# Down projection's S1 begun in gate and up, additions kept in order, residual rows loaded into place, the norm's second block scaled on VectorE

## The chip, the cores and the metric

One core of one Trainium2 chip runs the program. Its engines are TensorE (PE; its weight loads are shown as PEld), VectorE (DVE), ScalarE (ACT), GpSimd (POOL) and SyncE (SP). The first four compute; SP and POOL also start the DMAs that matter here. The metric is the device time of one execution in microseconds: 1347.09 us before the change, the median of 3 runs (1346.76 to 1351.79).

## The reference

Two decoder layers on x of shape (1, 512, 1024), all float32:

```
for each layer:
    p = x @ w_in                          # columns for two token mixers
    a = gated linear recurrence (4 heads x 128)
    b = sparse attention (8 heads x 64: compressed, selected and window branch)
    x = layer_norm(alpha*x + concat(a, b) @ w_out, ln1)
    h = silu(x @ w_ffn_gate) * (x @ w_ffn_up)        # 512 x 2816
    x = layer_norm(alpha*x + h @ w_ffn_down, ln2)    # alpha = sqrt(2)
```

The layer norm takes mean and variance over the 1024 columns, and then multiplies by a vector g and adds a vector b.

## The kernel before

Every matmul operand is split into a high and a low float32r half (a cast on ScalarE, then a subtraction on VectorE), and a product is three matmuls: high by high, high by low, low by high (`mm3`). The order of the instructions on each engine is fixed when the program is built: a planner walks a modelled timeline and takes, on each engine, the ready instruction of the highest priority, giving out the buffers of each tag as they come free. `high_priority(offset=3000)` moves an instruction ahead by 3000 places. On the chip every engine, and every DMA queue, then works in that fixed order.

The 512 rows stand as four tiles `rows[0]` to `rows[3]` of 128 x 1024, in two large buffers `R` (tag `a`, 11 buffers of 128 x 2048).

Output projection (`first_half`, `second_half`): the first half adds alpha times the old rows. Line 887 loads them in eight pieces of 128 x 512 into small tiles `xr` (tag `f`, three buffers), and line 888 scales them, adds PSUM and writes `rows`. `second_half` splits its third weight into two more buffers of `f`.

Norm (`norm_turn`): for two row tiles at a time, `norm_stats` gives the mean and 1/deviation, line 735 their product, and ScalarE scales both tiles in place (line 736). TensorE transposes them, and ScalarE applies g and b on the way to the next layer's operands (line 745). The rows themselves get g and b later, in `norm_rest`: a multiplication and an addition of 128 x 1024 for each of four tiles (lines 756 and 757). In gate and up this hangs on hook 3 of `seven`.

Gate and up (`seven`): twenty units, each two weight blocks combined with the halves of x by Strassen's scheme in seven products of 12 matmuls. `stage` loads a unit's weights with SyncE into tiles `a` (128 x 1024), `s1`, `s3` and `d`, and GpSimd adds to `s1` and `s3` by accumulating DMAs (lines 104 and 105). Tile `a` takes tag `wr` (two buffers), in every third unit `f` (in the third unit `pt`). Line 117 subtracts for the low halves, line 153 and line 162 make two more sums on VectorE.

Down projection: Strassen again, over four quarters q of the hidden columns. `first(q)` needs the sum S1 of two weight blocks: a load by SyncE (line 1036; line 1060 for q = 3) and an addition by GpSimd's queue (line 1038; 1061). Line 1074 adds a third block to the same tile for `third(q)`, and line 1087 a fourth for `fourth(q)`. The final loop needs one more sum, S3, in a buffer of `f` (line 1128), which comes free when the S1 tile that had it is done. GpSimd's queue takes all these additions in turn, each when its own load has landed and its readers are done.

Of the kernel before, what the change touches and what calls it, by code (L numbers as in the profile page):

```python
# [34 lines left out]
class Kern:  # L35
# [58 lines left out]
    def stage(self, sa, sb):  # L94

        nc = self.nc
        with self.tc.high_priority(offset=3000):
            self.turn += 1
            tag, bufs = ("wr", 2) if self.turn % 3 else ("pt", 2) if self.turn == 3 else ("f", 3)
            a = self.sb.tile([128, 1024], F32, name="wraw", tag=tag, bufs=bufs)  # L100
            s1, s3, d = (self.sb.tile([128, 512], F32, name=n, tag=t, bufs=2) for n, t in (("ws1", "st"), ("ws3", "pc"), ("wd", "wd")))
            nc.sync.dma_start(s1, sb[:, 512:])
            nc.sync.dma_start(s3, sa[:, :512])
            nc.gpsimd.dma_start(s1, sb[:, :512], accum_op=OP.add)
            nc.gpsimd.dma_start(s3, sb[:, :512], accum_op=OP.add)
            nc.sync.dma_start(a, sa)
            nc.sync.dma_start(d, sb[:, 512:])
        return a, s1, s3, d
# [17 lines left out]
    def seven(self, units, R, hooks):  # L126

        nc = self.nc
# [11 lines left out]
        for n, unit in enumerate(units + [None]):  # L140
# [8 lines left out]
            if unit:  # L149
                self.prod(D, s1, R["T1"], True)  # L150
                y = copy("sy", D)
                with self.tc.high_priority(offset=3000):
                    nc.vector.tensor_tensor(a[:, :512], s1, a[:, :512], op=OP.add)
                self.prod(B, a[:, 512:], R["R21"], True)
                unit[2]("11", B, x)
# [64 lines left out]
    def wide_mm(self, pts, w, xs, i, start, stop, by_tile=False):  # L220

        order = [(k, t) for k in range(2) for t in pts]
        if by_tile:
            order.sort(key=lambda kt: list(pts).index(kt[1]))
        for k, t in order:
            self.mm3(pts[t], *xs(2 * i + k, t), *w(k * 512, 512), start and k == 0, stop and k == 1)

    def xs_of(self, x):
# [499 lines left out]
    def norm_turn(self, l, which, b, rows, x, raw=None):  # L728
# [3 lines left out]
        for t in (2 * b, 2 * b + 1):  # L732
            mean, rs = self.norm_stats(t)
            nb = self.small(1, "nb", tag="l")
            nc.vector.tensor_scalar(nb, mean, rs, -1.0, op0=OP.mult, op1=OP.mult)
            nc.scalar.activation(rows[t], rows[t], AF.Identity, scale=rs, bias=nb)
        for k2 in range(0, NK, 2):
# [24 lines left out]
    def layer(self, l):  # L762
# [95 lines left out]
        def rblocks():  # L858
            R.extend(self.big("r") for _ in range(2))
            rows.extend(R[t // 2].rearrange("p a b -> p (a b)")[:, (t % 2) * 1024:(t % 2 + 1) * 1024] for t in range(NT))  # L860

        def quart(b, q):
# [13 lines left out]
        def first_half(c):  # L876

            def f():
                ws = [self.load_w(io["wo1"][l, c, i]) for i in range(2)]
                cs = slice(c * 512, (c + 1) * 512)  # L880
                for b in range(2):
                    pts = {t: self.ps("d") for t in (2 * b, 2 * b + 1)}
                    for i in range(2):
                        self.wide_mm(pts, ws[i], ysf, i, i == 0, i == 1)
                    xr = self.sb.tile([128, 2, 512], F32, name="xr", tag="f", bufs=3)
                    for e, (t, p) in enumerate(pts.items()):
                        nc.gpsimd.dma_start(xr[:, e], self.xres[t * 128:(t + 1) * 128, cs])
                        nc.vector.scalar_tensor_tensor(rows[t][:, cs], xr[:, e], ALPHA, p, op0=OP.mult, op1=OP.add)
            return f
# [115 lines left out]

        self.seven([(io[w][l, j], io[w][l, j + 1], f(j)) for j in range(2, NF, 2) for w, f in (("wg", gate), ("wu", up))], R,
                   {3: lambda: self.norm_rest(l, 0, rows, None)})

# [7 lines left out]
        def split(dst, src):  # L1016
            with tc.high_priority(offset=3000):
                nc.scalar.copy(dst[0], src)  # L1018
                nc.vector.tensor_tensor(dst[1], src, dst[0].bitcast(F32), op=OP.subtract)  # L1019

        def places(k):
# [11 lines left out]

        def raw_w(src, plus=None, tag=("wr", 2)):
            t = self.sb.tile([128, 1024], F32, name="wraw", tag=tag[0], bufs=tag[1])
            nc.sync.dma_start(t, src)
            if plus is not None:
                nc.gpsimd.dma_start(t, plus, accum_op=OP.add)
            return t

        def dprod(acc, w, r, start, stop):
# [8 lines left out]
        half = [[(H[2 * q + e][:, :, b * 256:(b + 1) * 256]) for e in range(2) for b in range(2)] for q in range(QS)]  # L1050
        sums, ops = {}, {}

        def first(q):

            with tc.high_priority(offset=3000):
                if q < 3:
                    s = raw_w(wd[1, 2 * q], wd[1, 2 * q + 1], ("f", 3))
                else:
                    s = self.big("ws").rearrange("p a b -> p (a b)")[:, :1024]
                    nc.sync.dma_start(s, wd[1, 2 * q])  # L1060
                    nc.gpsimd.dma_start(s, wd[1, 2 * q + 1], accum_op=OP.add)
            r11, r12, _, r22 = half[q]
# [6 lines left out]
            with tc.high_priority(offset=3000):  # L1069
                nc.vector.scalar_tensor_tensor(r11, t1, -1.0, r22, op0=OP.mult, op1=OP.subtract)  # L1070
            sums[q] = s
            dprod(Y, split_w(s), o1, q == 0, q == QS - 1)
            with tc.high_priority(offset=3000):
                nc.gpsimd.dma_start(s, wd[0, 2 * q], accum_op=OP.add)

# [5 lines left out]
        def third(q):  # L1081
# [4 lines left out]
            with tc.high_priority(offset=3000):  # L1086
                nc.gpsimd.dma_start(sums[q], wd[0, 2 * q + 1], accum_op=OP.add)

        def fourth(q):
            dprod(Z, split_w(sums[q]), ops["22", q], q == 0, q == QS - 1)  # L1090

        for f, q in ((first, 0), (first, 1), (second, 0), (first, 2), (third, 0), (second, 1), (first, 3), (third, 1),
                     (fourth, 0), (second, 2), (third, 2), (fourth, 1), (second, 3), (third, 3), (fourth, 2)):
            f(q)
# [28 lines left out]
        for q in range(QS):  # L1123
# [3 lines left out]
            with tc.high_priority(offset=3000):  # L1127
                s3 = raw_w(wd[0, i], wd[1, i], ("f", 3))
                p12, p22 = raw_w(wd[0, i + 1]), raw_w(wd[1, i + 1])
                nc.vector.tensor_tensor(r12, r22, r12, op=OP.subtract)  # L1130
# [5 lines left out]
            split(o4, r11)  # L1136
            dprod(Q, split_w(s3), o3, q == 0, end)
            dprod(M, split_w(p12), o21, False, False)
            if q == 0:
                fourth(QS - 1)  # L1140
            dprod(N, split_w(p22), o4, q == 0, end)
            if q == 0:
# [149 lines left out]
```

## Time and profile before

| | |
|---|---|
| median of 3 runs | 1347.09 us |
| the profiled execution | 1353.65 us |
| its span, first to last instruction | 1351.9 us |
| TensorE busy, share of the span | 1311.2 us, 97% |
| VectorE | 1012.4 us, 75% |
| ScalarE | 749.6 us, 55% |
| GpSimd | 192.5 us, 14% |
| mean granted TensorE clock | 0.989 of 2.4 GHz |
| moved by DMA | 186.54 MB, 138 GB/s |

Matmuls overlap, so a recorded matmul is longer than the step from one to the next, and a busy TensorE need not be at its peak. In the tables and chains below, "x" counts instructions, `out<-in` names tiles, and "<-" behind an idle time names what ended it. Layer 0 has gate and up from about 350 to 557 us and the down projection until about 670; layer 1 has them from about 1020 to 1227 and until the end.

### The profile page before, as it was taken

The page shows a single profiled execution, that of the slowest core. Times are in us where ns is not written, and L with a number is a line of the kernel's source. Part 1 is how long each engine was busy: PE and PEld are TensorE (multiplying, and loading weights), DVE is VectorE, ACT ScalarE, POOL GpSimd, SP SyncE. Part 2 cuts the span into 40 slices and gives each one's busy share as a digit, 9 for nine tenths or more (in the row PEclk, how much of TensorE's full clock was granted, in tenths as well). Part 3 has the DMA queues.
Part 4 walks back from the last instruction along what each step waited for, and adds up shares of the span by engine and source line. Part 5 has one row for each costly group of instructions (what it writes and reads, how often), then busy time and mean ns, then how long its engine had stood idle before and what let it go on. Part 6 is the DMA issues. An engine that isn't in the chain of part 4 may idle for free.

```text
span 1351.9 us, 23468 instructions
## 1 busy us (share of the span) xinstructions
PE 1311.2 (97%) x8853; PEld 1200.4 (89%) x8853; DVE 1012.4 (75%) x2021; ACT 749.6 (55%) x1495; POOL 192.5 (14%) x275
## 2 busy tenths in 40 slices
PE   8999999999999999999999999999999999999997
PEld 6988999789999999877899989987899999997776
DVE  4755798866887778967667668988559877788767
ACT  5254777844655555645452558777256555556530
POOL 1140111111011121110011100111010111111102
PEclk9999999999999999999999999999999999999999
DMA  7253212252467778586433221132515777866852
GB/s 236 79 164 102 79 56 74 84 161 76 149 167 185 189 189 197 136 223 174 152 140 116 73 92 63 63 102 71 166 29 179 178 184 180 215 158 150 213 196 79
DMA packets 67682, 186.54 MB, mean 138 GB/s; under 512 B 8175, under 2 KB 8351, under 8 KB 67056
## 3 DMA queue, kind: packets, MB, share of 16 engines
q1 hardware_dynamic: 44640, 124.73, 27.9%
q0 software_dynamic: 21920, 58.47, 21.2%
q10 hardware_dynamic: 1008, 1.84, 0.4%
q8 instruction: 69, 1.13, 0.3%
q14 instruction: 45, 0.37, 0.1%
HBM read 180.76 MB, written 7.10 MB: 139 GB/s over the span
## 4 chain that ended last, share of the span: by engine, by line
PE 59%; DVE 5%; DMA 5%; ACT 2%; issue 2%; POOL 0%; POOLq 0%; DVEq 0%; ACTq 0%
PE ps_d L83 10%; PE ps_d L82 10%; PE ps_d L84 10%; PE ps_t L84 3%; PE ps_t L82 3%; PE ps_t L83 3%; DMA wraw<-in_wd 3%; PE ps_s L82 2%; PE ps_s L83 2%; PE ps_s L84 2%; DMA ws<-in_wd 1%; PE ps_t L647 1%; DVE wlo L1019 1%; DVE hop L1019 1%; PE ps_h L390 1%
## 5 line engine op out<-in xcount | busy, mean ns | idle before, releaser
L116 ACT CAST whi<-wraw 128x512 fp32r<-128x512 f32 x160 | 98.6, 620 | 123.1 <-PE ps_d L83 93.3
L82 PE MATMUL ps_d<-xh,whi 128*128 128x256 f32 (+1 forms) x424 | 141.9, 338 | 2.0 <-ACT gates L497 1.2
L84 PE MATMUL ps_d<-xh,wlo 128*128 128x256 f32 (+1 forms) x424 | 142.6, 337 | 0.0
L83 PE MATMUL ps_d<-xl,whi 128*128 128x256 f32 (+1 forms) x424 | 141.7, 335 | 0.6 <-DVE mv L712 0.6
L117 DVE TENSOR_TENSOR wlo<-wraw,whi 128x512 fp32r<-128x512 f32 x160 | 108.9, 687 | 44.5 <-ACT whi L116 42.1
L84 PE MATMUL ps_d<-th,wlo 128*128 128x256 f32 x480 | 133.7, 284 | 2.4 <-DVE wlo L117 2.4
L83 PE MATMUL ps_d<-tl,whi 128*128 128x256 f32 x480 | 134.9, 283 | 0.0
L82 PE MATMUL ps_d<-th,whi 128*128 128x256 f32 x480 | 133.9, 283 | 0.1
L76 ACT CAST whi<-wraw 128x1024 fp32r<-128x1024 f32 (+1 forms) x68 | 70.7, 1040 | 97.0 <-PE ps_d L84 19.8
L77 DVE TENSOR_TENSOR wlo<-wraw,whi 128x1024 fp32r<-128x1024 f32 (+1 forms) x68 | 82.4, 1211 | 51.9 <-ACT whi L76 51.5
L84 PEld LDWEIGHTS ps_d<-th,wlo 128*128 128x128 f32 x480 | 91.2, 192 | 3.0 <-DVE wlo L117 3.0
L83 PEld LDWEIGHTS ps_d<-tl,whi 128*128 128x128 f32 x480 | 92.1, 192 | 0.1
L82 PEld LDWEIGHTS ps_d<-th,whi 128*128 128x128 f32 x480 | 91.4, 192 | 0.9 <-ACT su L136 0.5
L82 PEld LDWEIGHTS ps_d<-xh,whi 128*128 128x128 f32 x424 | 81.4, 193 | 9.2 <-ACT gates L497 1.3
L1019 DVE TENSOR_TENSOR wlo<-wraw,whi 128x1024 fp32r<-128x1024 f32 x50 | 60.6, 1219 | 38.3 <-ACT whi L1018 38.3
L83 PEld LDWEIGHTS ps_d<-xl,whi 128*128 128x128 f32 x424 | 81.9, 193 | 7.6 <-DVE mv L712 1.2
L84 PEld LDWEIGHTS ps_d<-xh,wlo 128*128 128x128 f32 x424 | 81.8, 193 | 7.5 <-DVE wlo L77 0.5
L83 PE MATMUL ps_d<-wlo,xh 128*128 128x256 f32 (+1 forms) x304 | 88.3, 291 | 0.0
L82 PE MATMUL ps_d<-whi,xh 128*128 128x256 f32 (+1 forms) x304 | 88.0, 291 | 0.0
L1018 ACT CAST whi<-wraw 128x1024 fp32r<-128x1024 f32 x50 | 52.3, 1051 | 64.1 <-DMA wraw<-in_wd 38.9
L84 PE MATMUL ps_d<-whi,xl 128*128 128x256 f32 (+1 forms) x304 | 87.8, 290 | 0.0
L608 ACT ACTIVATE e<-e,mn 128x128 f32<-128x128 f32 (+3 forms) x128 | 71.8, 564 | 22.1 <-DVE mn L606 21.7
(460 smaller groups left out, 4182.1 us busy)
## 6 DMA issues: line engine op xcount, KB each, us to landing
wraw<-in_wd SPq DMA_DIRECT2D x50, 512.0 KB, 4.2
wraw<-in_wf SPq DMA_DIRECT2D x31, 512.0 KB, 3.2
wraw<-in_wd POOLq DMA_DIRECT2D x26, 512.0 KB, 6.7
wraw<-in_wg SPq DMA_DIRECT2D x24, 512.0 KB, 3.9
wraw<-in_wu SPq DMA_DIRECT2D x24, 512.0 KB, 4.6
ws<-in_wg SPq DMA_DIRECT2D x40, 256.0 KB, 3.7
ws<-in_wg POOLq DMA_DIRECT2D x40, 256.0 KB, 4.7
ws<-in_wu SPq DMA_DIRECT2D x40, 256.0 KB, 3.6
```

What stands on the lines that cost most here:

```text
L76: nc.scalar.copy(h, raw[:, i:i + n])
L77: nc.vector.tensor_tensor(o, raw[:, i:i + n], h.bitcast(F32), op=OP.subtract)
L82: first = t.matmul(out, ah, bh, start=start, stop=False, **kw)
L83: t.matmul(out, ah, bl, start=False, stop=False, **kw)
L84: t.matmul(out, al, bh, start=False, stop=stop, **kw)
L116: nc.scalar.copy(h, raw)
L117: nc.vector.tensor_tensor(o, raw, h.bitcast(F32), op=OP.subtract)
L390: nc.tensor.matmul(p2[:, i], S[:, blk(i)], kq(128 * (i + 2), [[2 * w, n], [256 + w, 2], [1, w]]), start=True, stop=True)
L608: nc.scalar.activation(e, e, AF.Exp, bias=mn, scale=-1.0, accum_out=sm)
L647: nc.tensor.transpose(p[:, c:c + 128], E[qt][:, j * 128:(j + 1) * 128], self.ident)
L1018: nc.scalar.copy(dst[0], src)
L1019: nc.vector.tensor_tensor(dst[1], src, dst[0].bitcast(F32), op=OP.subtract)
```

## The change

Five edits:

- `seven` no longer uses the tag `f`: tile `a` is in `wr` in all units but the third. `stage` keeps its last SyncE load, its last GpSimd addition and (from line 153) its VectorE sum in `self.tail`.
- The S1 sums of the down projection are begun by hooks of `seven`: the load of quarter q at unit 10 + 2q, its addition one unit later, placed in their queues behind those of the unit before by a new function `after` (an order, no wait). Quarter 3 uses a large buffer.
- The norm's remainder in gate and up becomes eight single instructions, one at each of units 3 to 9 and one at unit 11 (a multiplication and an addition for each tile in turn), each behind the VectorE sum of the unit before. The parameters are loaded at unit 2.
- All additions to the sums keep the order of the program on GpSimd's queue, and S3 is in large buffers of its own, two quarters to a buffer; it is begun by `begin3`: quarters 0 and 1 before `fourth(0)` and `fourth(1)`, the others in the final loop.
- The residual rows are loaded into `rows` by four DMAs of 128 x 1024, in place of eight pieces; line 888 then works in place. In `norm_turn` the scalings get a high priority, and the second tile of block 0 is scaled by VectorE.

```diff
@@ stage
-            tag, bufs = ("wr", 2) if self.turn % 3 else ("pt", 2) if self.turn == 3 else ("f", 3)
-            a = self.sb.tile([128, 1024], F32, name="wraw", tag=tag, bufs=bufs)
+            tag = "pt" if self.turn == 3 else "wr"
+            a = self.sb.tile([128, 1024], F32, name="wraw", tag=tag, bufs=2)
...
-            nc.gpsimd.dma_start(s3, sb[:, :512], accum_op=OP.add)
+            add = nc.gpsimd.dma_start(s3, sb[:, :512], accum_op=OP.add)
             nc.sync.dma_start(a, sa)
-            nc.sync.dma_start(d, sb[:, 512:])
+            self.tail = [nc.sync.dma_start(d, sb[:, 512:]), add, None]
@@ seven
-                    nc.vector.tensor_tensor(a[:, :512], s1, a[:, :512], op=OP.add)
+                    self.tail[2] = nc.vector.tensor_tensor(a[:, :512], s1, a[:, :512], op=OP.add)
+    def after(self, a, b):
+        self.tc.add_manual_dep(a.ins, b.ins.name, mybir.DependencyInfo(
+            mybir.DependencyClass.NoSync, mybir.DependencyReason.DATA), reason="queue order")
@@ norm_turn
-            nc.vector.tensor_scalar(nb, mean, rs, -1.0, op0=OP.mult, op1=OP.mult)
-            nc.scalar.activation(rows[t], rows[t], AF.Identity, scale=rs, bias=nb)
+            with self.tc.high_priority(offset=4000):
+                nc.vector.tensor_scalar(nb, mean, rs, -1.0, op0=OP.mult, op1=OP.mult)
+                if b == 0 and t % 2:
+                    nc.vector.tensor_scalar(rows[t], rows[t], rs, nb, op0=OP.mult, op1=OP.add)
+                else:
+                    nc.scalar.activation(rows[t], rows[t], AF.Identity, scale=rs, bias=nb)
@@ rblocks, first_half
+            for t in range(NT):
+                nc.gpsimd.dma_start(rows[t], self.xres[t * 128:(t + 1) * 128, :])
...
-                    xr = self.sb.tile([128, 2, 512], F32, name="xr", tag="f", bufs=3)
-                    for e, (t, p) in enumerate(pts.items()):
-                        nc.gpsimd.dma_start(xr[:, e], self.xres[t * 128:(t + 1) * 128, cs])
-                        nc.vector.scalar_tensor_tensor(rows[t][:, cs], xr[:, e], ALPHA, p, op0=OP.mult, op1=OP.add)
+                    for t, p in pts.items():
+                        o = rows[t][:, cs]
+                        nc.vector.scalar_tensor_tensor(o, o, ALPHA, p, op0=OP.mult, op1=OP.add)
@@ gate and up, down projection
-                   {3: lambda: self.norm_rest(l, 0, rows, None)})
+        def add_w(t, src):
+            d = nc.gpsimd.dma_start(t, src, accum_op=OP.add)
+            self.after(d, self.tail[1])
+            self.tail[1] = d
...
+        def begin(q):
+            sums[q] = self.sb.tile([128, 1024], F32, name="wsum", tag="f", bufs=3) if q < 3 else halves("ws")[0]
+            self.after(nc.sync.dma_start(sums[q], wd[1, 2 * q]), self.tail[0])
+        def go_on(q):
+            add_w(sums[q], wd[1, 2 * q + 1])
+        def rest(i):
+            r, c = rows[i // 2], i % 2 * 1024
+            self.after(nc.vector.tensor_tensor(r, r, lnps[0][:, c:c + 1024], op=OP.add if i % 2 else OP.mult), self.tail[2])
+        hooks = {10 + 2 * q + e: lambda q=q, f=f: f(q) for q in range(QS) for e, f in enumerate((begin, go_on))}
+        hooks[2] = lambda: lnps.append(self.ln_params(l, 0))
+        for i in range(2 * NT):
+            hooks[i + 3 if i < 7 else 11] = lambda h=hooks.get(i + 3 if i < 7 else 11, lambda: None), i=i: (h(), rest(i))
...
-                nc.gpsimd.dma_start(s, wd[0, 2 * q], accum_op=OP.add)
+                add_w(sums[q], wd[0, 2 * q])
...
-                nc.gpsimd.dma_start(sums[q], wd[0, 2 * q + 1], accum_op=OP.add)
+                add_w(sums[q], wd[0, 2 * q + 1])
+        def begin3(q):
+            if q % 2 == 0:
+                s3s.extend(halves("ws3"))
+            with tc.high_priority(offset=3000):
+                nc.sync.dma_start(s3s[q], wd[0, 2 * q])
+                add_w(s3s[q], wd[1, 2 * q])
-                     (fourth, 0), (second, 2), (third, 2), (fourth, 1), (second, 3), (third, 3), (fourth, 2)):
+                     (begin3, 0), (fourth, 0), (second, 2), (third, 2), (begin3, 1), (fourth, 1), (second, 3), (third, 3),
+                     (fourth, 2)):
...
-                s3 = raw_w(wd[0, i], wd[1, i], ("f", 3))
+            if q < QS - 2:
+                begin3(q + 2)
```

## Rows read from the trace of the kernel before

**Rows 1.** Windows: us, busy of each engine (count), granted clock, DMA share, GB/s.

```profile
375.00:545.00 170.00, 170.00 (x1419) 170.00 (x1418) 133.92 (x240) 95.48 (x196) 30.16 (x35) 1.00 0.76 188
553.00:656.00 103.00, 98.77 (x441) 79.75 (x441) 78.93 (x100) 51.57 (x66) 12.32 (x15) 0.98 0.75 193
```

**Rows 2.** TensorE's waits, whole span: total us, times, longest us.

```profile
PE ps_t L82 <- ACT whi L1018: 5.7, 3, 2.2
...
PE ps_d L82 <- DVE r L888: 2.9, 2, 2.3
...
PE ps_s L82 <- ACT whi L1018: 1.6, 3, 0.6
```

**Rows 3.** TensorE's waits from 355 to 375 us, gate and up of layer 0.

```profile
PE ps_t L82 <- ACT whi L116: 0.9, 1, 0.9
PE ps_d L84 <- DVE wlo L117: 0.8, 1, 0.8
PE ps_t L84 <- DVE wlo L117: 0.6, 1, 0.6
```

**Rows 4.** TensorE's waits from 1028 to 1052 us, gate and up of layer 1.

```profile
PE ps_d L84 <- DVE wlo L117: 1.6, 2, 1.2
PE ps_t L82 <- DVE h_at L978: 1.1, 1, 1.1
```

**Rows 5.** Timeline of VectorE from 360 us: start us, us, instruction, count.

```profile
361.05 4.62 DVE L756 TENSOR_TENSOR r<-r,lnp 128x1024 f32<-128x1024 f32 x4
365.59 0.68 DVE L162 TENSOR_TENSOR wraw<-wraw 128x512 f32<-128x512 f32 x1
```

**Rows 6.** Timeline of TensorE from 606 us, around the hole before `fourth(3)`.

```profile
607.45 0.40 PE L84 MATMUL ps_o<-whi,hop 128*128 128x512 f32 x1
...
612.35 0.63 PE L83 MATMUL ps_t<-wlo,hop 128*128 128x512 f32 x1
```

**Rows 7.** Timeline of GpSimd from 568 us, the additions of the down projection.

```profile
571.17 0.86 POOL L1087 DMA_DIRECT2D wraw<-in_wd  x1 [1.76 <-DVE wlo L1019]
...
598.09 0.85 POOL L1038 DMA_DIRECT2D wraw<-in_wd  x1 [10.09 <-DMA wraw<-in_wd]
598.63 1.20 POOL L1087 DMA_DIRECT2D ws<-in_wd  x1
```

**Rows 8.** Timeline of VectorE from 590 us, the split of quarter 3's sum.

```profile
592.19 1.23 DVE L1019 TENSOR_TENSOR wlo<-ws,whi 128x1024 fp32r<-128x1024 f32 x1 [0.89 <-ACT whi L1018]
```

**Rows 9.** Timeline of ScalarE from 575 us, the splits for `fourth(0)` and `fourth(3)`.

```profile
579.24 1.04 ACT L1018 CAST whi<-wraw 128x1024 fp32r<-128x1024 f32 x1 [4.64 <-DMA wraw<-in_wd]
...
608.76 1.04 ACT L1018 CAST whi<-ws 128x1024 fp32r<-128x1024 f32 x1 [5.78 <-DMA ws<-in_wd]
```

**Rows 10.** Windows of 3.4 us behind the wait for line 888.

```profile
962.20:965.60 3.40, 1.33 (x5) 1.09 (x6) 3.17 (x4) 0.16 (x1) 0.00 (x0) 0.92 0.24 59
965.60:969.00 3.40, 3.40 (x12) 2.68 (x11) 1.26 (x2) 1.04 (x1) 0.00 (x0) 0.57 0.73 249
```

**Rows 11.** Timeline of VectorE from 950 us, first half of the output projection.

```profile
962.39 1.23 DVE L77 TENSOR_TENSOR wlo<-wraw,whi 128x1024 fp32r<-128x1024 f32 x1 [5.36 <-ACT whi L76]
963.53 0.68 DVE L888 SCALAR_TENSOR_TENSOR r<-xr,ps_d 128x512 f32<-128x512 f32 x1
```

**Rows 12.** Timeline of ScalarE from 950 us, same place.

```profile
955.21 1.05 ACT L76 CAST wx<-wraw 128x1024 fp32r<-128x1024 f32 x1 [1.89 <-DVE r L888]
```

**Rows 13.** Groups by line and form, ScalarE: busy us, mean ns, idle before.

```profile
L736 ACT ACTIVATE r<-r,nb,rstd 128x1024 f32<-128x1024 f32 x12 | 14.9, 1244 | 18.6 <-DVE nb L735 18.3
```

**Rows 14.** Groups by line and form, VectorE.

```profile
L345 DVE TENSOR_SCALAR hgF<-hgF,lbv 128x512 f32<-128x512 f32 x4 | 2.2, 545 | 3.2 <-ACT hgF L342 3.2
```

**Rows 15.** Line 106 from 380 to 545 us, the loads of `a`.

```profile
DMA to landing us min/median/max: 3.5/5.0/6.3
```

**Rows 16.** Line 116 from 380 to 545 us: what ended its idle time, longest.

```profile
  PE ps_d L83: 50.1, 47
```

**Rows 17.** Timeline of SyncE's queue from 545 us.

```profile
556.07 0.33 SPq L1060 DMA_DIRECT2D ws<-in_wd  x1
```

More of the change, by code (lines that the diff above doesn't have):

```diff
@@ L1004, in up @@
             return take
-        self.seven([(io[w][l, j], io[w][l, j + 1], f(j)) for j in range(2, NF, 2) for w, f in (("wg", gate), ("wu", up))], R,
-                   {3: lambda: self.norm_rest(l, 0, rows, None)})
         QS = 4
@@ L1019, in split, with raw_w, halves @@
                 nc.vector.tensor_tensor(dst[1], src, dst[0].bitcast(F32), op=OP.subtract)
+        def raw_w(src):
+            t = self.sb.tile([128, 1024], F32, name="wraw", tag="wr", bufs=2)
+            nc.sync.dma_start(t, src)
+            return t
+        def add_w(t, src):
+            d = nc.gpsimd.dma_start(t, src, accum_op=OP.add)
+            self.after(d, self.tail[1])
+            self.tail[1] = d
+        def halves(name):
+            b = self.big(name).rearrange("p a b -> p (a b)")
+            return [b[:, :1024], b[:, 1024:]]
+        sums = {}
+        def begin(q):
[3 more added lines that the diff above has]
+            add_w(sums[q], wd[1, 2 * q + 1])
+        lnps = []
+        def rest(i):
[5 more added lines that the diff above has]
+            hooks[i + 3 if i < 7 else 11] = lambda h=hooks.get(i + 3 if i < 7 else 11, lambda: None), i=i: (h(), rest(i))
+        self.seven([(io[w][l, j], io[w][l, j + 1], f(j)) for j in range(2, NF, 2) for w, f in (("wg", gate), ("wu", up))], R, hooks)
         def places(k):
@@ L1032, in split_w @@
             return w
[L1034 to L1039, printed above, removed]
         def dprod(acc, w, r, start, stop):
@@ L1050, in layer @@
         half = [[(H[2 * q + e][:, :, b * 256:(b + 1) * 256]) for e in range(2) for b in range(2)] for q in range(QS)]
-        sums, ops = {}, {}
+        ops, s3s = {}, []
         def first(q):
[L1055 to L1061, printed above, removed]
             r11, r12, _, r22 = half[q]
@@ L1070, in first @@
                 nc.vector.scalar_tensor_tensor(r11, t1, -1.0, r22, op0=OP.mult, op1=OP.subtract)
-            sums[q] = s
-            dprod(Y, split_w(s), o1, q == 0, q == QS - 1)
+            dprod(Y, split_w(sums[q]), o1, q == 0, q == QS - 1)
             with tc.high_priority(offset=3000):
-                nc.gpsimd.dma_start(s, wd[0, 2 * q], accum_op=OP.add)
+                add_w(sums[q], wd[0, 2 * q])
         def second(q):
@@ L1136, in layer @@
             split(o4, r11)
-            dprod(Q, split_w(s3), o3, q == 0, end)
+            dprod(Q, split_w(s3s[q]), o3, q == 0, end)
             dprod(M, split_w(p12), o21, False, False)
```

## The prediction

> **What bounds the kernel now.** I read the table by stage first. In gate and up, TensorE and its weight loads are both busy for the whole stretch, 1419 matmuls in 170.0 us or 0.120 us each, at the full 2.4 GHz level [rows 1]; nothing can be gained there, only lost. VectorE is at 133.9 of these 170 us, the DMA engines at a share of 0.76. In the down projection TensorE has 4.2 us of recorded idle time in 103 [rows 1]. The list of TensorE's waits then says what is late when it stops: the high half of a weight in the down projection (5.7 and 1.6 us), the eviction of line 888 (2.9 us) [rows 2], and early in gate and up the splits of lines 116 and 117, 2.3 us in layer 0 and 2.7 us in layer 1 [rows 3, 4]. So the change can win only by closing such holes, some 13 us of waits, and what a hole drags behind it: after the one at 962 us the granted clock of the next 3.4 us is 0.57, so most of it ran at 1.2 GHz [rows 10]. The two slices lose (0.08 + 0.43) x 3.4 = 1.7 us.
>
> **The sum** is made against the profiled execution, 1353.65 us (span 1351.9, and 1.75 around it). It lies 0.49% above the median of 1347.09, so the forecast is scaled by the ratio at the end.
>
> *The norm's remainder, spread over gate and up.* Before, eight VectorE instructions per layer (four multiplications, four additions, 128x1024) come nearly together: four take 4.62 us from 361.05, and the sum of line 162, which a split and then TensorE need, starts only at 365.59 [rows 5]. That is where the 2.3 us of layer 0 come from; layer 1 has the same pattern. Now one of the eight follows each of eight blocks. A block is 84 matmuls of 0.120 = 10.1 us; VectorE does 133.9/170 of that, 7.9 us, and with 1.2 us more 9.1, still under 10.1. Gain at most 2.3 + 2.7 = 5.0 us; if every layer has one addition fall ahead of a late split instead, -2.4 us. I take 4.5, near the top, because the work around is otherwise unchanged. The load of the norm's parameters is issued one block ahead of its first reader; its cover is that block.
>
> *S1 begun in gate and up, S3 in buffers of its own, additions in order.* The S1 sums of quarters 0 to 2 were already loaded in gate and up, in buffers of the tag `f`. Only quarter 3's was not: SyncE issues its load at 556.07 [rows 17]. The larger effect is at the other end. Quarter 3's sum is read for the third product by 592.19 + 1.23 = 593.4 us [rows 8], and its next addition could start then. GpSimd issues it at 598.63, because the addition for S3 stands ahead of it at 598.09, after 10.09 us of waiting for its own load [rows 7]. It lands 10.1 us after its issue, when ScalarE can start, 608.76 [rows 9]. TensorE began its last matmul before the hole at 607.45 and its sixth from there at 612.35 [rows 6]: 4.9 us for five matmuls of 0.23, so 3.75 us lost, and 1.7 us by the clock as above. With S3's load begun earlier, in a buffer that nobody has to free first, the addition goes at 593.5 and lands by 603.6 even at 10.1 us, 3.9 us ahead of 607.45. Gain 5.4 us in layer 0. In layer 1 the same order holds but the hole is small: of the 1.6 us on `ps_s` 0.4 is layer 0's, 1.2 remains. Together 6.6. What is late next is the fourth product of quarter 0: its addition is issued at 571.17 and ScalarE waits for it until 579.24, 8.1 us [rows 7, 9]. Its issue hangs on a backlog of VectorE that the change leaves, so I give 0.5 us for the transfers of quarter 3 that are gone from beside it. The bound above is both layers' whole wait there, 5.7 - 2.0 = 3.7 us, and 1.7 of clock. The bound below is -4 us: S3's loads, 512 KB each, come to lie beside the additions, and each of two holes per layer grows by 1 us.
> The buffer for quarter 3's S1 is one of the large ones that the operand splits use early. Two 0.68 us VectorE subtractions per layer (that size: line 162, rows 5) then move into the crowded start of the down projection; 4 x 0.68 = 2.7, of which I take half, -1.4.
>
> *The gate and up weights lose the `f` buffers.* The first weight of every block now takes turns in two buffers. I cost it at nothing. A buffer is held while six products are fed, 6 x 12 x 0.120 = 8.6 us, and refilled in 5.0 us (3.5 to 6.3) [rows 15], 13.6 of the 20.2 us of two blocks. And ScalarE, at the head of every split, waited in the whole stretch for TensorE to free the halves (50.1 us on the largest line), never for a DMA [rows 16]. If that cover is gone, the second rival below begins.
>
> *Residual rows straight into place.* Eight loads of 256 KB per layer become four of 512 KB, on GpSimd's queue, behind which stand the strips and the small powers of the norms; they start when the old activations' buffers come free. The wait on line 888 is not one for the residual, though: at 962.39 VectorE takes a weight split that waited 5.36 us for ScalarE, and line 888 stands behind it at 963.53 [rows 11]. ScalarE was waiting there for the weight's load; before that, at 955.21, it had waited 1.89 us for a buffer that line 888 gives back [rows 12]. With the `f` buffers free this second wait goes, and eight transfers no longer lie beside the late load. But the place behind the split may stay. Above: 2.9 us and 1.7 of clock, 4.6; below: -1 us, if GpSimd holds up a strip. I take half of the upper end, 2.3, since it is the buffer and not the order that I see go.
>
> *The norm's second tile scaled on VectorE.* It takes 1.24 us on ScalarE [rows 13], three times in the program. VectorE needs 0.545 us for 128x512 with two scalars [rows 14]; for 128x1024 between that and the 1.16 us of a two-tensor pass (4.62/4, rows 5). An estimate of 0.8 us, the middle, gives 3 x 0.44 = 1.3 us at most, if the transposes move up with it; below it is -1.5, when it delays the additions of the other block. I take 1.0.
>
> Sum: 4.5 + 6.6 + 0.5 - 1.4 + 0 + 2.3 + 1.0 = 13.5 us. 1353.65 - 13.5 = 1340.15, a ratio of 0.990, and 0.990 x 1347.09 = 1334 us. Its own range is 1326 to 1340.4.
>
> **The rivals.**
> *The holes move but stay.* The order on each engine is laid out anew by the planner. If the operand split takes the large buffer first, quarter 3's S1 starts where it did; line 888 keeps its place; a hole at the fourth product comes back one product later. For it: 8.1 us for an addition that nothing blocked. Against it: GpSimd's 5.2 us of needless waiting is plainly the order of two additions. Only the first term is left, 4.5 us, and 0.5: 1342 us.
> *Gate and up starve: the other side.* The blocks' weights, with two buffers, wait for transfers that the S1 loads and additions lengthen. The place is blocks 10 to 18. It decides when a weight takes over 20.2 - 8.6 = 11.6 us from the release of its buffer to its landing; an addition needs 10.1 us today [rows 7, 9], a weight at most 6.3 [rows 15]. If it is exceeded by 3 us per pair of blocks, in the five pairs from block 10 on, 15 us a layer, 30 in all: 1353.65 - 13.5 + 30 = 1370, scaled 1363; with half of that 1348. Against it: three of the four S1 sums are loaded in that stretch today without a wait.
> The Trainium skill (DMA: Bandwidth & Descriptors, section Issuing engines are not separate DMA queues) speaks for this rival: transfers started from different engines run on the same 16 DMA engines and interleave, so a second queue buys no bandwidth. By that rule moving a transfer into a stretch with a share of 0.76 is paid by its neighbours there; the trace shows how full the stretch is [rows 1], and no row of it shows the price.
> *All holes of the down projection's first half close*, with the fourth product's in both layers (5.4 - 0.5) and all of line 888 (2.3 more): 7.2 us better, 1327 us.
>
> **How the numbers follow.** Forecast 0.47, holes stay 0.28, starved 0.16, all closed 0.09. A measurement of this kernel can tell 0.5%, 6.7 us, from no change: faster is under 1340.4, slower over 1353.8. Faster: nearly all of the forecast (0.43), a fifth of the second (0.05), the last (0.09): 0.57. Slower: three quarters of the starved case (0.12) and a little of the second (0.01): 0.13. Within: the rest, 0.30. The terms' upper bounds add up to 22.9 us gained (5.0 + 6.6 + 3.7 + 1.7 + 4.6 + 1.3), 1324 us; the lower ones to 11.6 us lost (2.4 + 4 + 2.7 + 1 + 1.5), 1359. The range 1322 to 1354 goes 2 us below the first, since the three runs shown scatter over 5 us, and leaves out about 0.03 there and 0.13 at the slow end.
>
> **What would show it.** The additions and multiplications of the norm one to a block, and no TensorE wait in the first 25 us of gate and up: first term. Quarter 3's S1 loaded before the end of gate and up, its last addition issued within 1 us of its third split, and no hole at some 607 us: second. Fewer or shorter waits on the eviction of the residual: third. The prediction is wrong if ScalarE's casts in gate and up show waits for a DMA, if TensorE takes more than 170 us for 1419 matmuls there, or if the time stays above 1341 with the holes closed.

## The result, and the profile after

The changed kernel takes 1336.78 us (median of 6, 1333.94 to 1337.39) against 1349.86 us before (median of 6): ratio 0.9901, 95% interval 0.9882 to 0.992. Forecast were 1334 us and 1322 to 1354. The profiled execution took 1336.99 us (span 1335.2).

Span and mean granted clock of TensorE in three profiles: before, after, and a later version, `f2_later`, told of below.

```profile
core 0: 1351.9 us, clock 0.989
```

```profile
core 0: 1335.2 us, clock 0.995
```

```profile
core 0: 1328.7 us, clock 0.998
```

How the second number is read matters: over 78 executions of the kernel before it lay between 0.986 and 0.999, with 0.9925 as the mean, so the same program differs by up to 1.3% by it. Below I therefore give, beside each ratio, the difference in **span times granted clock**, the time that the execution would have had at the full level. It is a worked-out measure (not all of a span hangs on TensorE), but it scatters far less: 1338.5 us for the kernel before, standard deviation 1.9 over the 78; 1327.7 after, 1.2 over 6. So 10.8 us (95%: 9.7 to 12.0) of the gain are work and waits, and the clock's mean, 0.9948 after, goes with the rest, some 3 us. The 78 ran on four chips, whose means lie between 1338.3 and 1338.8 us, so this measure can be compared from chip to chip.

Windows of the kernel after, as [rows 1] (us; busy of PE, PEld, DVE, ACT, POOL with counts; clock; DMA share; GB/s). The down projection is some 5 us shorter in this profile, so its window ends earlier:

```profile
375.00:545.00 170.00, 170.00 (x1419) 170.00 (x1419) 138.21 (x241) 95.70 (x194) 31.05 (x36) 1.00 0.78 198
553.00:651.00 98.00, 95.33 (x430) 78.01 (x429) 80.42 (x102) 51.75 (x65) 11.40 (x14) 1.00 0.72 187
```

Gate and up feeds the same 1419 matmuls in 170 us: nothing starved. TensorE's waits, whole span, after (total us, times, longest):

```profile
PE ps_h L82 <- ACT whi L1026: 2.3, 2, 1.1
...
PE ps_s L83 <- DVE wlo L1027: 1.4, 2, 0.7
...
PE ps_d L82 <- ACT whi L1026: 1.1, 2, 0.6
```

The waits of `ps_t` on the weights' high half and those on the residual's eviction [rows 2] are gone, and so are those of lines 116 and 117 [rows 3, 4]. The three lines shown are new: 2.4 us in each layer at the start of the down projection. The waits of the mixers and norms are still there (the largest is 5.4 us, 4.6 before). VectorE in gate and up, the first and last of the norm's eight instructions (start, us), against four in a row of [rows 5]:

```profile
369.81 1.22 DVE L1057 TENSOR_TENSOR r<-r,lnp 128x1024 f32<-128x1024 f32 x1
...
449.06 1.22 DVE L1057 TENSOR_TENSOR r<-r,lnp 128x1024 f32<-128x1024 f32 x1
```

GpSimd's additions in the down projection, as [rows 7] (last: idle before, and what ended it):

```profile
570.47 0.86 POOL L1036 DMA_DIRECT2D wsum<-in_wd  x1 [0.25 <-DVE wlo L1027]
576.35 0.85 POOL L1036 DMA_DIRECT2D ws<-in_wd  x1 [5.02 <-DVE wlo L1027]
578.09 0.84 POOL L1036 DMA_DIRECT2D wsum<-in_wd  x1 [0.89 <-DVE wlo L1027]
578.62 1.18 POOL L1036 DMA_DIRECT2D ws<-in_wd  x1
...
592.44 0.85 POOL L1036 DMA_DIRECT2D ws<-in_wd  x1 [6.44 <-DVE wlo L1027]
```

The reader is to look at the releasers: each addition for a due product waits for the split that frees its buffer (VectorE), none for another transfer's load. The S3 addition (578.62) goes right behind a due one, and quarter 3's last (592.44) goes as soon as its third split is done, where before it went at 598.63 [rows 7]; no hole is left where [rows 6] had one. SyncE's load of quarter 3's S1, and ScalarE's split of that quarter's sum for the fourth product (556.07 and 608.76 before [rows 17, 9]):

```profile
494.32 0.42 SPq L1048 DMA_DIRECT2D ws<-in_wd  x1
```

```profile
601.80 1.06 ACT L1026 CAST whi<-ws 128x1024 fp32r<-128x1024 f32 x1 [2.15 <-DMA ws<-in_wd]
```

### The profile page after: what moved, and what is told of

It is laid out like the page before. It is cut to its first block, busy times and chain, and to the rows that moved or that the text cites. A ratio compares the mean times of both kernels' runs of the same rounds, so it can differ in the third digit from the quotient of the medians.

```text
span 1335.2 us, 23431 instructions
## 1 busy us (share of the span) xinstructions
PE 1303.4 (98%) x8853; PEld 1197.8 (90%) x8853; DVE 1015.6 (76%) x2024; ACT 748.0 (56%) x1492; POOL 186.5 (14%) x267
## 3 DMA queue, kind: packets, MB, share of 16 engines
q0 software_dynamic: 21792, 58.47, 21.1%
## 4 chain that ended last, share of the span: by engine, by line
PE 87%; DVE 5%; DMA 2%; ACT 2%; issue 2%; POOL 1%; POOLq 0%; DVEq 0%; ACTq 0%
PE ps_d L82 16%; PE ps_d L83 16%; PE ps_d L84 15%; PE ps_t L82 4%; PE ps_t L84 4%; PE ps_t L83 4%; PE ps_s L83 3%; PE ps_s L84 3%; PE ps_s L82 3%; PE ps_t L652 2%; PE ps_h L395 2%; PE ps_o L663 1%; PE ps_o L662 1%; PE ps_s L524 1%; PE ps_o L84 1%
## 5 line engine op out<-in xcount | busy, mean ns | idle before, releaser
L611 DVE CUSTOM_DVE_ANT_0 e<-ps_s,strip 128x128 f32<-128x128 f32 (+3 forms) x128 | 59.1, 485 | 16.0 <-PE ps_s L626 12.9
L116 ACT CAST whi<-ws 128x512 fp32r<-128x512 f32 x80 | 49.5, 618 | 24.5 <-ACT sy L136 11.4
```

Source lines behind the costliest of these rows:

```text
L116: nc.scalar.copy(h, raw)
L611: nc.vector.tensor_tensor_reduce(out=e, in0=pa, in1=st[:, 512 - pa.shape[-1]:], scale=1.0, scalar=3e38, op0=OP.add, op1=OP.min, accum_out=mn)
```

## The experiments

All were timed in five rounds beside the kernel before on the same chip. "At full clock" is the difference in span times granted clock to the 78 executions of before, with its 95% half-width.

| kernel | ratio, 95% interval | at full clock, us |
|---|---|---|
| after | 0.9901 (0.9882 to 0.992) | -10.8 ±1.1 |
| before + norm spread (`p1_spread`) | 0.9962 (0.994 to 0.9984) | -4.5 ±1.5 |
| before + S1/S3/order (`p2_down`) | 0.9967 (0.9944 to 0.9991) | -3.6 ±1.2 |
| before + residual rows (`p3_resid`) | 1.0011 (0.9992 to 1.003) | -0.4 ±1.1 |
| before + norm's scaling (`p4_norm`) | 0.9997 (0.997 to 1.0023) | -0.4 ±1.1 |
| after, scaling as before (`m1_normold`) | 0.9907 (0.9883 to 0.9932) | -10.3 ±1.3 |
| after, residual as before (`m5_resold`) | 0.9898 (0.9875 to 0.9922) | -9.4 ±1.0 |
| after, S3 as before (`m3_s3old`) | 0.9973 (0.9959 to 0.9986) | -0.6 ±1.1 |
| after, additions not ordered (`m4_noorder`) | 0.9984 (0.9963 to 1.0004) | -4.0 ±1.1 |
| after, S1 in the first products (`m2b_s1old`) | 0.9921 (0.989 to 0.9952) | -8.1 ±1.6 |
| after, S1 held to the end (`m2_s1late`) | 1.0167 (1.0141 to 1.0192) | +10.2 ±0.9 |
| after + loop's subtractions later (`f2_later`) | 0.9875 (0.9847 to 0.9904) | -13.2 ±0.8 |
| the same + products held (`f4_hold`) | 0.9882 (0.9857 to 0.9907) | -14.0 ±1.0 |

### Each edit alone

`p1_spread`:

```
-   {3: lambda: self.norm_rest(l, 0, rows, None)})
+   hooks = {i + 3 if i < 7 else 11: lambda i=i: rest(i) ...}   # one instruction per block
```

> The kernel before with one edit: the norm's eight additions and multiplications one to a block. Theory (from the two traces, stage by stage): the wait on lines 116 and 117 early in gate and up goes, 1.0 us in layer 0 and 3.2 in layer 1, so 4.2 us less, ratio 0.997, and no TensorE wait in the first 25 us of gate and up. Rival (the gain of those stages came from the S1 transfers or from the freed residual loads): the wait stays, time within 1 us of before.

Measured: 4.5 us at full clock, and between 350 and 380 and between 1010 and 1052 us TensorE waits for nothing. Theory held.

`p2_down`:

```
-   tag, bufs = ("wr", 2) if self.turn % 3 else ("pt", 2) if self.turn == 3 else ("f", 3)
+   tag = "pt" if self.turn == 3 else "wr"
+   hooks: begin(q), go_on(q) at blocks 10 + 2 * q and 11 + 2 * q; add_w with its order; begin3 in "ws3"
+   hooks[3] = lambda: self.norm_rest(l, 0, rows, None)          # the other edits as before
```

> The kernel before with the S1/S3 edit alone (S1 begun in gate and up, S3 in buffers of its own, additions in one order, staging buffers given up). Theory: the down projections lose 6.4 and 6.6 us and the dips of the clock there, 13 us, ratio 0.990, with no TensorE hole at the fourth products of quarters 0 and 3. Rival 1 (the prediction's own terms): 5.7 us, ratio 0.996. Rival 2 (part of the 13 us came from VectorE being freed by the other edits): 6 to 10 us, ratio 0.993 to 0.996, with the hole at the fourth product of quarter 0 still there.

Measured: 3.6 us at full clock, 4.5 by the ratio, near rival 1; my theory fell. It had read 13 us from two profiles, before and after, of which the clock's dips in those stages were part. The profile of `p2_down` keeps 0.9 us at quarter 0's fourth product in layer 0, and has 1.8 us of waits at the start of each down projection (0.3 before). How loosely a hole hangs on one addition shows in `p4_norm`, another build whose down projection is untouched. There too an addition for S3 waits 8.02 us for its load, with quarter 3's behind it at 600.96, 2 us after its third split (599.0). Yet the profile has no hole at some 607 us, and 3.0 us instead at quarter 0's fourth product:

```profile
600.42 0.85 POOL L1042 DMA_DIRECT2D wraw<-in_wd  x1 [8.02 <-DMA wraw<-in_wd]
600.96 1.20 POOL L1091 DMA_DIRECT2D ws<-in_wd  x1
```

```profile
584.29 0.74 PE L82 MATMUL ps_t<-whi,hop 128*128 128x512 f32 x2 [3.00 <-ACT whi L1022]
```

`p3_resid`:

```
+   for t in range(NT): nc.gpsimd.dma_start(rows[t], self.xres[t * 128:(t + 1) * 128, :])
-   nc.vector.scalar_tensor_tensor(rows[t][:, cs], xr[:, e], ALPHA, p, ...)
+   nc.vector.scalar_tensor_tensor(o, o, ALPHA, p, ...)                    # o = rows[t][:, cs]
```

> The kernel before with the residual rows loaded straight into place, and nothing else. Theory: the wait on line 888 and the clock dip behind it in layer 1 go, 3.0 us less, and 0.2 in layer 0: ratio 0.9976. Rival (the wait was the place behind a late split, which only the freed staging buffers or the new order moved): within 1 us of before, with the wait on that line still 2 to 3 us.

`p4_norm`:

```
+   if b == 0 and t % 2: nc.vector.tensor_scalar(rows[t], rows[t], rs, nb, ...)
+   else: nc.scalar.activation(rows[t], ...)                              # high priority
```

> The kernel before with the second row tile of the norm's first block scaled on VectorE, at high priority, and nothing else. Theory: from the last product of the output projection to the first product of gate and up takes 1.2 us more in each layer, 2.4 us more in all, ratio 1.002. Rival 1 (the prediction's term): 1.0 us less. Rival 2 (the 1.2 us came from other instructions that the new order put ahead of the norm, not from VectorE's scaling): no change, 0.999 to 1.001.

Both theories fell; of the rivals, only `p4_norm`'s second (no change) held. The residual's wait is gone in `p3_resid`, yet the kernel isn't faster. TensorE's last product of the output projection and first of gate and up, layer 0, with the residual edit alone (compare 323.20 to 326.18 in the kernel before, 2.98 us):

```profile
321.74 0.28 PE L84 MATMUL ps_d<-whi,y 128*128 128x256 f32 x1
...
325.95 0.80 PE L82 MATMUL ps_d<-xh,whi 128*128 128x256 f32 x2
```

That is 4.21 us with ScalarE scaling both tiles, and `p4_norm` has 2.97: what I had put down to VectorE's scaling came with the residual. With the rows in place the planner takes products of the second half (256 columns) as filler earlier: 23 of those into `ps_s` ran from 317.3 to 320.1 us before, and here all are done by 293.2. That they are missing where the norm of block 0 needs cover was the reading; `f4_hold`, below, tests it.

### The changed kernel with one part taken back

`m1_normold` has the scaling of before, `m5_resold` the eight loads of before (the two diffs above, reversed).

> The changed kernel with the norm's scaling as before (both row tiles on ScalarE, no priority of its own). Ratio against the kernel before. Theory now (residual rows alone gave the 1.2 us longer way into gate and up, the scaling alone gave none): the way from the last product of the output projection to the first of gate and up stays near 4.2 us, time within 2 us of the changed kernel, ratio 0.989 to 0.992. Rival 1 (VectorE's scaling costs what I first read from the two traces): 3.0 us there, 2.4 us faster, ratio 0.988. Rival 2 (with the residual in place the scaling on VectorE saves the prediction's 1 us): 5 us there, ratio 0.991 to 0.992.

> The changed kernel with the residual loaded as before, in eight loads through the buffers f. Ratio against the kernel before. Theory: the first product of gate and up comes 3.0 us after the last of the output projection again, not 4.2, in both layers (2.4 us faster), and the holes on the eviction of line 888 come back (0.8 us in layer 0, 2.4 in layer 1, and some of the clock behind the second); the two nearly cancel, within 2 us of the changed kernel, ratio 0.989 to 0.992. Rival 1 (the freed f buffers were what the eviction waited for): no holes there either, 2.4 us faster, ratio 0.988. Rival 2 (the prediction's term): 2.3 us slower, ratio 0.992.

Both theories held: each is within 2 us of the changed kernel. The scaling can't be told from nothing (0.5 ±1.6 us). The residual taken back costs 1.5 ±1.4 us, at the edge, and the ratio doesn't show it (0.9898 to 0.9901). In `m1_normold` the way is 4.20 us. In `m5_resold` it is 2.98 us again, and the holes on line 888's successor are back, 0.8 and 1.9 us; but its profile also has 1.9 us at quarter 0's fourth product, which the edit doesn't touch.

`m3_s3old`:

```
-   nc.sync.dma_start(s3s[q], wd[0, 2 * q]); add_w(s3s[q], wd[1, 2 * q])     # begin3
+   s3 = self.sb.tile([128, 1024], F32, name="wraw", tag="f", bufs=3)        # in the loop
+   nc.sync.dma_start(s3, wd[0, i]); nc.gpsimd.dma_start(s3, wd[1, i], accum_op=OP.add)
```

> The changed kernel with S3 as before: in a buffer of the tag f, its load and its addition issued at high priority in the loop of the last products, its addition not ordered among the others; S1 still begun in gate and up. Ratio against the kernel before. Theory: the addition for S3 stands again ahead of quarter 3's last one on GpSimd, the hole at some 607 us and its pair in layer 1 come back, 3 to 6 us, ratio 0.993 to 0.995. Rival (S1 begun early is what closed it): no hole there, ratio 0.989 to 0.992.

Measured: 10.3 us slower than the changed kernel at full clock, above the theory's 3 to 6. GpSimd's timeline of this kernel, and TensorE's longest hole:

```profile
584.89 0.85 POOL L1159 DMA_DIRECT2D wraw<-in_wd  x1 [8.14 <-DMA wraw<-in_wd]
585.43 1.19 POOL L1036 DMA_DIRECT2D wsum<-in_wd  x1
596.74 0.85 POOL L1159 DMA_DIRECT2D wraw<-in_wd  x1 [10.12 <-DMA wraw<-in_wd]
597.27 1.19 POOL L1036 DMA_DIRECT2D ws<-in_wd  x1
```

```profile
597.05 0.73 PE L82 MATMUL ps_t<-whi,hop 128*128 128x512 f32 x2 [1.99 <-ACT whi L1026]
```

This is [rows 7] again, twice: line 1159, the addition for S3, waits 8.14 and 10.12 us for its own load, and the due addition stands 0.5 us behind it. In the kernel before it happened for quarter 3 alone; S1 begun early did not undo it. The hole didn't come back where the theory put it: TensorE waits at quarter 2's fourth product (the line above) and for two later weights (0.7 and 1.1 us), and not at quarter 3's fourth.

`m4_noorder`:

```
-   d = nc.gpsimd.dma_start(t, src, accum_op=OP.add); self.after(d, self.tail[1]); self.tail[1] = d
+   nc.gpsimd.dma_start(t, src, accum_op=OP.add)
```

> The changed kernel without the tie that keeps the additions in their written order on GpSimd; S3's buffers and S1's early begin stay. Ratio against the kernel before. Theory A (the prediction's step: the order of two additions made the hole): an addition for S3 is issued ahead of a due one again and a hole of 1 us or more comes back at a fourth product in each layer, ratio 0.992 to 0.995. Theory B (S3's own, early buffer is what counts, since its addition then never waits for its load): no hole, within 2 us of the changed kernel, ratio 0.989 to 0.992.

Theory A held, and the price is above it: 6.8 ±1.5 us to the changed kernel; by the ratio, the whole change without the order can't be told from none (at full clock 4.0 us are left). Now the planner issues S3's additions ahead of quarter 0's last one. GpSimd, and then ScalarE's split for that quarter's fourth product:

```profile
565.30 0.85 POOL L1036 DMA_DIRECT2D ws<-in_wd  x1 [2.77 <-PE ps_o L84]
567.89 0.85 POOL L1036 DMA_DIRECT2D ws<-in_wd  x1 [1.73 <-DMA ws<-in_wd]
569.04 2.02 POOL L1036 DMA_DIRECT2D wsum<-in_wd  x2
```

```profile
582.18 1.05 ACT L1026 CAST whi<-wsum 128x1024 fp32r<-128x1024 f32 x1 [8.24 <-DMA wsum<-in_wd]
```

GpSimd is hardly held up here, 1.73 us; but the due addition, the second of the last line, is issued at 569.6 and takes 12.5 us to land. In the changed kernel the same one is issued at 570.47, lands 7.3 us later, and is split at 577.86, not waiting for it. The order is the only edit, and it puts two S3 additions of 512 KB each ahead; that these lengthen the due transfer is the reading, not tested by moving them alone. TensorE waits 2.7 us for it. At quarter 3 the old picture is back as well:

```profile
596.12 0.84 POOL L1036 DMA_DIRECT2D ws<-in_wd  x1 [7.01 <-DMA ws<-in_wd]
598.83 1.72 POOL L1036 DMA_DIRECT2D ws<-in_wd  x2 [1.87 <-DMA ws<-in_wd]
```

```profile
PE ps_t L82 <- ACT whi L1026: 3.9, 2, 2.7
```

The third split of that quarter is done at 597.2; its last addition is the second of the pair at 598.83, issued at 599.4 behind two for S3 that waited 7.01 and 1.87 us for their loads, and the hole at its fourth product is 1.2 us (layer 0's list, above). The Trainium skill (DMA: Bandwidth & Descriptors, section Issuing engines are not separate DMA queues) says that transfers started from any engine run on the same 16 DMA engines and interleave; the 12.5 us against 7.3 agree with it, and it is here that its price shows, where I had looked for it in gate and up.

`m2_s1late` and `m2b_s1old` begin S1 in the first products' program part:

```
 def first(q):
+    with tc.high_priority(offset=3000): begin(q); go_on(q)    # m2b: with no tie to tail[0], tail[1]
```

> The changed kernel with S1 begun where the kernel before begins it, in the down projection's program part; S3's buffers and the order of the additions stay. Ratio against the kernel before. Theory (the gain of the down projection is the order of the additions, and S3 out of the way; quarters 0 to 2 were loaded early anyway): the hole at the fourth product of quarter 3 stays closed, time within 2 us of the changed kernel, ratio 0.989 to 0.992. Rival (beginning S1 early is what frees the start of the down projection): the down projections are 3 us longer each, ratio 0.994 to 0.996.

> The changed kernel with the loads of S1, and their additions, put where the kernel before has them: in the first products' program part, at high priority and tied to nothing, so that the planner is free to pull them forward (the run before this one, m2_s1late, kept the ties to the last block's transfers and so held them back to the end of gate and up). S3's buffers and the order of the later additions stay. Ratio against the kernel before. Theory (S3's own buffers closed the holes at the fourth products; the early S1 of quarter 3 takes a large buffer from the operand splits, and their subtractions then make the new holes at the start of the down projection, 2.9 us a layer): those holes shrink to the 0.5 us of the kernel before, the fourth products stay without a hole, 3 to 5 us faster than the changed kernel, ratio 0.986 to 0.988. Rival 1 (beginning S1 early, with its order, is needed for the fourth products too): holes of 1.5 us or more there, ratio 0.992 to 0.997. Rival 2 (it makes no difference): 0.989 to 0.991.

`m2_s1late` was a bad test of the kernel before: its ties held S1 behind the last block's transfers. It shows what a late S1 costs: three waits, 16.0 us together, in layer 0, and 21 us in all against the changed kernel.

```profile
PE ps_s L82 <- ACT whi L1026: 16.0, 3, 6.9
```

`m2b_s1old` parts the theory. The recorded waits at the start of the down projection do shrink, from 2.4 us a layer to 0.2. (The expectations count these holes from start to start of the matmuls, which gives 2.9.) But the fourth product of quarter 0 waits again, 1.7 and 2.4 us:

```profile
583.50 0.73 PE L82 MATMUL ps_t<-whi,hop 128*128 128x512 f32 x2 [1.67 <-ACT whi L1026]
```

Its addition is issued at 571.50, 1.0 us later than in the changed kernel, and takes 10.8 us instead of 7.3; quarter 3's S1 is now loaded and added in the same stretch (its addition is issued at 562.36 and takes 9.0). It is 2.8 ±1.8 us slower than the changed kernel: rival 1.

### The holes that the change made, and a faster version

The changed kernel at the start of the down projection: TensorE (562.29 is its first product there), and VectorE before the low half it waits for.

```profile
565.89 0.39 PE L84 MATMUL ps_o<-whi,hop 128*128 128x512 f32 x1
567.41 0.50 PE L82 MATMUL ps_h<-whi,hop 128*128 128x512 f32 x1 [1.14 <-ACT whi L1026]
567.75 0.40 PE L82 MATMUL ps_o<-whi,hop 128*128 128x512 f32 x1
567.98 0.39 PE L82 MATMUL ps_d<-whi,hop 128*128 128x512 f32 x1
569.09 0.50 PE L83 MATMUL ps_s<-wlo,hop 128*128 128x512 f32 x1 [0.72 <-DVE wlo L1027]
```

```profile
562.40 1.22 DVE L1027 TENSOR_TENSOR wlo<-wraw,whi 128x1024 fp32r<-128x1024 f32 x1
563.54 0.42 DVE L1013 SCALAR_TENSOR_TENSOR h_e<-up,h_e 128x256 f32<-128x256 f32 x1
563.88 0.69 DVE L1166 TENSOR_TENSOR h_qs<-h_qs 128x512 f32<-128x512 f32 x1
564.48 0.69 DVE L1171 SCALAR_TENSOR_TENSOR h_at<-h_at 128x512 f32<-128x512 f32 x1
...
567.82 1.22 DVE L1027 TENSOR_TENSOR wlo<-wsum,whi 128x1024 fp32r<-128x1024 f32 x1
```

By 563.5 TensorE has fed the high halves of two sums; their low halves aren't made, so their buffers stay taken, ScalarE's next cast has to wait for the weight that ends at 565.89 (1.14 us of TensorE's time), and then the low half itself is late (0.72). Its cast was done at 562.1; VectorE comes to it at 567.82. Among what stands between are two subtractions, lines 1166 and 1171, that nobody needs before some 600 us. `f2_later` holds them back:

```
-   nc.vector.tensor_tensor(r12, r22, r12, op=OP.subtract)
+   self.after(nc.vector.tensor_tensor(r12, r22, r12, op=OP.subtract), lows[7 + q])
```

and line 1171 likewise; `lows` are the low halves in program order.

> The changed kernel with one thing more: the two subtractions by which each quarter of the last products' loop prepares its operands (lines 1166 and 1171) are held behind the low half of a later weight, so that they no longer run at the crowded start of the down projection. Ratio against the kernel before. Theory (the 2.9 us of holes there are VectorE's backlog, and three of these eight 0.69 us subtractions stand in it): the holes shrink by 1 to 2.5 us a layer, 2 to 5 us faster than the changed kernel, ratio 0.987 to 0.989. Rival (the wait is ScalarE's for a buffer of the high halves, as the list of waits names it, and not VectorE's backlog): holes unchanged, ratio 0.989 to 0.992, or slower if the subtractions are late for the loop.

Theory held. Its VectorE runs the same split at 560.60, 2.6 us behind TensorE's first product (557.97) instead of 5.5, TensorE goes from one product to the next without a wait there, and its PE list for 1208 to 1320 us is empty:

```profile
560.60 1.23 DVE L1027 TENSOR_TENSOR wlo<-wsum,whi 128x1024 fp32r<-128x1024 f32 x1
```

It is 2.4 ±1.3 us faster than the changed kernel at full clock; the ratios' intervals overlap. The recorded waits of both down projections fall from 5.1 to 2.9 us. What is left are holes of 0.3 to 0.9 us in layer 0, most of them new (0.72 us at 593.32, at a fourth product).

`f4_hold` adds a tie in the output projection:

```
+   m = self.tok_mm(..., held.get(0) if b == 1 and q == 2 else None)   # behind block 0's last quarter
```

> The kernel of f2_later with one thing more: in the output projection, the products of row block 1's third quarter are held behind the last quarter of row block 0, so that they can't be used up early. (With the residual in place the planner runs these 24 products, and others like them, some 10 us earlier, as filler; in the kernel before they stand behind row block 0's last quarter and cover its norm.) Ratio against the kernel before. Theory (the 1.2 us longer way into gate and up comes from this missing cover, not from VectorE's scaling): the way from the output projection's last product to the first of gate and up falls from 4.2 to 3.0 us in both layers, 2.4 us faster than f2_later, ratio 0.985 to 0.987. Rival 1 (the filler is missed where it was taken from): a hole on the eviction of the residual comes back in the output projection, 1 us or more a layer, ratio 0.987 to 0.989. Rival 2 (the norm's chain itself sets those 4.2 us): nothing changes, 0.9865 to 0.9885 with 4.2 us still there.

TensorE, layer 0: last product of the output projection, first of gate and up.

```profile
327.37 0.37 PE L84 MATMUL ps_d<-whi,y 128*128 128x256 f32 x1
...
330.27 0.61 PE L82 MATMUL ps_d<-xh,whi 128*128 128x256 f32 x2
```

The way falls to 2.90 us in both layers, as the theory of the missing cover has it, and rival 2 falls. But the time doesn't follow (0.8 us to `f2_later`, within both half-widths; by the ratio it is no faster): the stretch from there to the first product of block 1's operands grows from 19.6 to 21.2 us in layer 0 and from 19.5 to 21.1 in layer 1. From the output projection's last product to that point the two layers together take 48.7 us before, 48.7 after, 47.5 in `f2_later` and 48.0 in `f4_hold`. So the 1.2 us was no loss in the changed kernel: I had stopped the clock at a milestone instead of at the next point where TensorE's work is the same. In `p3_resid` the same stretch takes 50.2 us; that may be where the gain from its closed wait went, but no run shows why it is longer there.

## Why the prediction was right

**The total** was right, and so were its first term and the nothing for the staging buffers. The second term came out right by luck, since two errors in it cancelled. The last two terms, 3.3 us, aren't shown by the edits alone. The four edits alone add up to 8.9 us; the 1.9 ±2.7 us to the measured 10.8 can't be told from nothing.

*The norm's remainder, 4.5 us:* right in place and size, 4.5 ±1.5 alone. One instruction per block, no wait early in gate and up. One reading was wrong: 1.1 of layer 1's 2.7 us [rows 4] wait for line 978, not for the splits of lines 116 and 117; they went as well.

*S1, S3 and the order, 6.6 + 0.5 - 1.4 = 5.7 us:* of this 1.7 was clock (from 600 to 625 us it was 0.93 before and 1.00 after, which is as much), and the measure at full clock leaves it out; the other 4.0 agree with 3.6 ±1.2 alone, and the 5.7 with 4.5 by the ratio (1.2 to 7.6). The pieces don't agree. The step "GpSimd issues it at 598.63, because the addition for S3 stands ahead of it" is borne out by `m3_s3old` and `m4_noorder`, which bring back the row on GpSimd and the loss. But S3's part is worth 10.3 ±1.5 us in this kernel and not 7.1: other fourth products hang on it too, quarter 2's (`m3_s3old`) and quarter 0's (`m4_noorder`). The two terms that failed are the 0.5 and the -1.4. The first was for quarter 0's fourth product: its waits, 1.4 and 2.2 us before, are all gone. The second was "half" of four subtractions moved into the start of the down projection, with a bound of -2.7: the recorded waits there are 2.4 us a layer against 0.3 before, 4.2 us together. I had priced the moved instructions by their own durations and not by the backlog of VectorE that they join. `f2_later` shows that this backlog is the cause, and `m2b_s1old` that the early S1 brings it. The two holes also trade places: a TensorE held up at the start comes later to quarter 0's fourth product, and in `m2b_s1old`, where the start is free, that product waits again. Up to and with that product, recorded waits are 1.7 and 2.6 us before and 2.4 and 2.4 after, so the two terms together, -0.9, were near.

*The staging buffers, nothing:* right. 1419 matmuls in 170 us; ScalarE's longest idle time on line 116 still ends with TensorE freeing a half (44.4 us, 50.1 before [rows 16]), and none of it with a DMA.

*The residual, 2.3 us:* too high. The wait went, as said ("the buffer and not the order"), but the edit alone gives 0.4 ±1.1, and taking it back costs 1.5 ±1.4. The rows in place changed what the planner uses as filler, which no step of mine had asked.

*The norm's scaling, 1.0 us:* can't be told from zero (0.4 ±1.1 alone, 0.5 ±1.6 taken back). VectorE needs 0.80 us for it (322.82 in the profile after), as estimated, against 1.22 for a two-tensor pass of that size:

```profile
322.82 0.80 DVE L743 TENSOR_SCALAR r<-r,rstd,nb 128x1024 f32<-128x1024 f32 x1
```

By the Trainium skill (VectorE: DVE Perf Modes, section Mode 2×_2P) an fp32 operation with one tensor operand in SBUF may run at twice the rate of one with two; the two rows point the same way, at a ratio of 1.5.

The rivals: "gate and up starve" is refuted by the windows. "All holes close" is half true: the old ones did, and new ones came. What I can't settle is the clock's share: the mean rose from 0.9925 to 0.9948, but with six executions after, and a range of 0.986 to 0.999 before, how much of the 3 us is the change's doing stays open. That long holes cost clock as well is shown by `m2_s1late`: 0.9827 in the mean.

## What to carry to other kernels

Accumulating transfers on one queue are a schedule: an addition that waits for its own load holds up the due one behind it, and beside others issued too early a due one took 12.5 us instead of 7.3; keep them in the order in which their products come. Work that is moved to a stretch where an engine is already late can cost the backlog, not its duration alone; fillers with no due date belong behind the due work. Before a difference of two profiles is given to an edit, run the edit alone, and compare stretches that end where the remaining work is the same.

## What the runs showed of the hardware that was not expected

The granted clock of one and the same program varied from 0.986 to 0.999 between executions, some 17 us if all of the span hung on it; against the 78, a dozen executions tell the span to about ±2.1 us, and span times clock to ±1.1 (standard deviations 3.4 and 1.9 us). An addition of 512 KB took from 5.1 to 13.1 us from issue to landing in the down projection of the changed kernel (layer 0).
